# A two-layer streaming encoder on one Trainium2 core: modulation columns fetched by GpSimd's queue, three buffers for the halves, sums ordered behind products, steps dealt anew

## The chip, the cores and the metric

The kernel runs on one core of a Trainium2 chip. The engines of that core work from separate instruction queues and wait for each other through semaphores: TensorE (PE in the profile; PEld is its weight load), VectorE (DVE), ScalarE (ACT), GpSimd (POOL) and SyncE (SP). SP and POOL can issue transfers between the chip's memory (HBM) and the core's on-chip memory; the transfers of both run on the same 16 DMA engines. The metric is the device time of one execution in microseconds.

## The reference

The input is 512 tokens of width 2048. There are two layers. Each normalises the stream, scales and shifts it with values computed from a conditioning vector `c`, runs a mixer, normalises the result and adds it back times a gate:

```python
sc = jax.nn.silu(c)
for l in range(2):
    mod = sc @ ada_w[l] + ada_b[l]                  # 2048 -> 3 * 2048
    shift, scale, gate = split(mod, 3)
    h = rmsnorm(x, g_pre[l]) * (1 + scale) + shift
    if l == 0:
        y = mlstm_mixer(h, ...)                     # a_w_in, 8 heads, then @ a_w_out (4096 -> 2048)
    else:
        kmod = sc @ kv_ada_w + kv_ada_b             # 2048 -> 2 * 2048
        hkv = rmsnorm(x, kv_g) * (1 + kmod_scale) + kmod_shift
        k, v = split(hkv @ kv_w, 2)
        y = band_attention_mixer(h, k, v, b_w_in, b_rel, b_w_out)
    x = x + gate * rmsnorm(y, g_post[l])
```

What matters here is `sc @ ada_w`: one vector of 2048 numbers times matrices of 2048 x 6144 (twice) and 2048 x 4096, all in float32. It is a matrix-vector product, 128 MB of matrix that is read once.

## The kernel before

**Matrix products.** All products are float32 in three parts: each operand is split into a high part (rounded by ScalarE's cast) and a low part (VectorE's subtraction), and TensorE adds high times high, high times low and low times high. The weights come in the order in which they are used, in pieces of 128 x 1024 numbers (512 KB): SP's queue loads a piece (`raw_load`, L227; tile `wr`), ScalarE casts it (`wh`, L211), VectorE subtracts (`wl`, L211), and TensorE's 24 matmuls of 512 columns use it (L276). Three buffers each hold `wr`, `wh` and `wl`, so weights can be ready at most two pieces ahead of the one in use.

**Modulation.** One column of `mod` is one 128 x 2048 block of the matrix (a transposed `ada_w`), multiplied by the broadcast `sc` and summed along its row: a single VectorE instruction per block (CUSTOM_DVE_ANT_0 in the profile, ISA in the order of instructions, each followed by a short read of the sum). The first 32 columns are done at the start. 48 more, whole blocks of 1 MB (tile `ada`), run in the background of the first three heads of layer 0: `background(n)` sums what was loaded before and loads the next one, two or three blocks, into three buffers. The last 48 are done in halves of 128 x 1024 (512 KB, tile `adh`) during the output product of layer 0 (`a_w_out`), with the half of `sc` that belongs to them in a tile `scH` of its own (`half_sums_step`, L1071 to L1088): 96 halves, two to a step, in two buffers. A step first sums the two halves that the step before loaded, then loads two more.

**Where the steps sit.** The output product runs over four groups of 512 columns; the first three take 16 pieces each, the last is done twice, for two token pairs. A table of k indices deals a step to a piece: every second piece in the first group, 15 pieces of 16 in the second and third, four in the first half of the last. The remaining seven steps lie in the key projections (`proj_s` on `kv_w`), after the values.

**What sets the order.** A scheduler orders each engine's instructions by the place where the program issues them; `high_priority(AHEAD)` lets the preparation of weights go ahead of its place, and `pin` keeps an instruction in the order of the program among the pinned ones. In this kernel the loads of columns are pinned in SP's queue, together with those of weights, and the sums are pinned on VectorE. An engine runs its queue in order: VectorE cannot subtract a weight piece while the sum in front of it waits for its block, and SP cannot issue a load while the load in front of it waits for a buffer.

**Other names.** `ps_y` are the sums of the output product, `y` its input tiles (fetched from scratch as `yr`), `sqy` the squares that empty a bank of sums (L996) behind `y` (L995). `xr` are rows of the input for the residual (L1011), `xn` normalised rows before they are turned (L1034), both in the pool `t2` of seven buffers of 2 KB a partition. `ps_s`, `e` and L800 are the scores of an mLSTM head.

Of the kernel before, what the change touches and what calls it, by code (L numbers as in the profile page):

```python
# [9 lines left out]
F32 = mybir.dt.float32  # L10
# [144 lines left out]
def hybrid_trunk(ctx, tc, xT, xN, c, adaT, cols, wst, wg, ext, kc, out):  # L155
# [9 lines left out]
    def pool(name, bufs=1, **kw):  # L165
        return tc.tile_pool(name=name, bufs=bufs, reuse_waits="tile", **kw)
# [31 lines left out]
    def col(i):  # L198
        return cl[:, i : i + 1]
# [30 lines left out]
    def wpiece(mat, groups=(), pl=None, bufs=(2, 2), early=False):  # L230
# [41 lines left out]
                out.append((sh, sl))  # L272
        return out

    def mm(ps, a, b, start, stop):
        return nc.tensor.matmul(ps, a, b, start=start, stop=stop)  # L276

    def mm3(ps, ah, al, bh, bl, start, stop):
        mm(ps, ah, bh, start, False)
# [209 lines left out]
    acp = hst.enter_context(pool("acc"))  # L489
    st = ExitStack()  # L490
    sp = st.enter_context(pool("start"))
    def ada_load(i, p, n, pin=lambda ins: ins, parts=1, js=None):

        w = D // parts
        js = range(parts) if js is None else js
        at = p.tile([P, w * len(js)], F32, tag="ada", name=f"ada{i}_{js[0]}", bufs=n)
        for j in js:
            c = (j - js[0]) * w
            pin(nc.sync.dma_start(at[:, c : c + w], adaT[i, :, j * w : (j + 1) * w]))
        return i, at, w, js  # L500

    def ada_sum(i, at, w, js, pin=lambda ins: ins, sc=None):
        for j in js:
            c = at[:, (j - js[0]) * w : (j - js[0] + 1) * w]
            pin(nc.vector.tensor_tensor_reduce(  # L505
                c, c, (sc or scB)[:, j * w : (j + 1) * w], 1.0, mod[:, i : i + 1] if j else col(CB + i),
                ALU.mult, ALU.add, mod[:, i : i + 1]
            ))
# [229 lines left out]
    pending = list(cols_left)  # L738
    loaded = []

    def background(n):

        for a in loaded:
            ada_sum(*a, tc.keep_in_program_order)
        loaded.clear()
        for b, i in enumerate(pending[:n]):
            loaded.append(ada_load(i, *((ap_, 2) if b < 2 else (bp, 1)), tc.keep_in_program_order))
        del pending[:n]

    def add_at(at, more):  # L750
# [204 lines left out]
    kst = ExitStack()  # L955
    kp = kst.enter_context(pool("kp", bufs=KT))
    tst = ExitStack()
    tp = tst.enter_context(pool("t2", bufs=7, side="right"))
    cqst = ExitStack()
    cp = cqst.enter_context(pool("cq"))  # L960
    rst = ExitStack()
# [98 lines left out]
    def rows(g, ms, xs, at={}, pl=None):  # L1060
        ps = [newp(f"ps_y0_{g}_{m}") for m in ms]
        proj_b("a_w_out", xs, ps, ms=ms, kts=32, at=at)
        with tc.high_priority(AHEAD):
            for p, m in zip(ps, ms):
                yt[m].append((pl or rp).tile([P, S], F32, tag="t" if pl else "r", name=f"y{m}_{g}"))
                evac(p, m, g, yt[m][g])
# [4 lines left out]
    def half_sums_step():  # L1071

        for i, j, a in halves:
            pin(nc.vector.tensor_tensor_reduce(  # L1076
                a, a, sc[1], 1.0, mod[:, i : i + 1] if j else col(CB + i), ALU.mult, ALU.add, mod[:, i : i + 1]
            ))
        halves.clear()
        for i, j in cols_left[:2]:  # L1080
            d = slice(j * 2 * S, (j + 1) * 2 * S)
            if sc[0] != j:
                sc[:] = j, cp.tile([P, 2 * S], F32, tag="sc", name=f"scH{i}_{j}")
                pin(nc.sync.dma_start(sc[1], csc[0, d].partition_broadcast(P)))
            a = cp.tile([P, 2 * S], F32, tag="adh", name=f"adh{i}_{j}", bufs=2)
            pin(nc.sync.dma_start(a, adaT[i, :, d]))
            halves.append((i, j, a))
        del cols_left[:2]  # L1088

    def steps_at(*ks):  # L1090
        return {k: half_sums_step for k in ks}

    gate_row(0, 0)
    rows(0, range(4), y_tile, steps_at(*range(2, 32, 4)))
    for g in (1, 2):
        gate_row(0, g)
        rows(g, range(4), ys, steps_at(*range(0, 30, 2)))
    gate_row(0, 3)
    rows(3, PAIRS[0], ys, steps_at(2, 10, 18, 26), tp)
    at = {2: lambda: residual(0), 4: lambda: residual(1)}  # L1100
    at |= {14 + 4 * i: lambda i=i: turned(0, [i]) for i in range(4)}
    rows(3, PAIRS[1], ys, at)
# [46 lines left out]
    for pair, ms in enumerate(PAIRS):  # L1149
        for g in range(2):  # L1150
            turn = {2 + 4 * i: lambda i=i: turned(1, [i]) for i in range(4)} if pair == 0 and g == 1 else {}
            if pair:
                turn = {k: input_sums for k in (2, 6, 12)}
            values(g, ms, turn)
    rst.close()
    zst = ExitStack()
    zp = zst.enter_context(pool("zp", bufs=2, side="right"))
    zxst = ExitStack()
    zx = zxst.enter_context(pool("zx", side="right"))
    for i in range(KT // 2):  # L1160
        z = zp.tile([P, 4, 256], F32, tag="z", name=f"zk{i}")
        ready = len(hs)
        at = {2: input_sums} if ready < KT // 2 else {}
        if i == 0:
            amul_cols(2, 48 + KT, GPRE + KT)
        if 0 < i:
            at[1] = half_sums_step
        assert ready == KEY_PAIRS[i]
        proj_s("kv_w", hkv, hs, ready, z[:, 0:2, :], z[:, 2:4, :], f"k{i}", zx, (2, 2), at, True, BANKS[i % 2])
        nc.sync.dma_start(ksc[i].rearrange("p a t -> p (a t)"), z.rearrange("p a t -> p (a t)"))  # L1170
    assert not cols_left and not halves
    zxst.close()
    cqst.close()
    kst.close()
    ast = ExitStack()
    kq = ast.enter_context(pool("kq"))
# [255 lines left out]
```

## Time and profile before

| | before |
|---|---|
| median of 3 runs | 2781.33 us (2780.82 to 2786.57) |
| the profiled execution | 2783.93 us, its span 2781.8 us |
| mean granted TensorE clock | 0.997 |
| TensorE busy | 2733.4 us (98%) |
| VectorE busy | 2281.7 us (82%) |
| ScalarE busy | 1402.9 us (50%) |
| GpSimd busy | 0.2 us, 4 instructions |
| DMA, SP's queue | 504.71 MB, 53.9% of 16 engines |
| DMA, GpSimd's queue | none |

TensorE is the engine with most work, and its idle time is 48 us in all, so what an edit can win is bounded by when and why TensorE waits. The view by stage (busy time of every engine in given stretches) finds where; the view of waits and the timeline of a few microseconds tell why. A busy share of a transfer queue is the share of the time of all 16 DMA engines.

### The profile page before, as it was taken

To read this page: it belongs to the slowest core of one execution; us is meant where nothing else is said; L and a number is where in the kernel's file an instruction comes from. 1 tells how busy PE (TensorE), PEld (TensorE's weight loads), DVE (VectorE), ACT (ScalarE), POOL (GpSimd) and SP (SyncE) were. 2 spreads that over 40 slices of the span, in tenths; PEclk is the share of its full clock that TensorE was granted. 3 is DMA by queue.
4 is the path that set the end of the run, shared out by engine and by line. 5 is a ranking of instruction groups with operands and counts; after the bars stand their busy time and mean duration, and the time that the engine had idled before them with its cause. 6 is when DMAs were issued, how large, how long until landed. Compare 5 with 4: busy or idle time off the path is not lost.

```text
span 2781.8 us, 44822 instructions
## 1 busy us (share of the span) xinstructions
PE 2733.4 (98%) x17551; PEld 2485.8 (89%) x17551; DVE 2281.7 (82%) x3655; ACT 1402.9 (50%) x2011; POOL 0.2 (0%) x4
## 2 busy tenths in 40 slices
PE   8999999999999999999999989899999999999998
PEld 6887888899999999999998868677998899999887
DVE  8977979989899898998987555677997788989625
ACT  4243533556565565555655211377534566666523
POOL 0000000000000000000000000000000000000000
PEclk9999999999999999999999999999999999999999
DMA  9757787223333233332338777889655544444455
GB/s 368 293 202 266 255 330 254 95 95 121 114 108 116 94 122 115 107 116 95 121 122 277 247 248 251 272 297 301 202 189 192 178 129 125 123 130 129 167 160 177
DMA packets 158095, 507.57 MB, mean 182 GB/s; under 512 B 16902, under 2 KB 30758, under 8 KB 147386
## 3 DMA queue, kind: packets, MB, share of 16 engines
q1 hardware_dynamic: 157882, 504.71, 53.9%
q8 instruction: 137, 2.24, 0.3%
q14 instruction: 76, 0.61, 0.1%
HBM read 471.03 MB, written 38.85 MB: 183 GB/s over the span
## 4 chain that ended last, share of the span: by engine, by line
PE 81%; DMA 10%; DVE 5%; issue 2%; ACT 1%; SPq 0%; DVEq 0%; ACTq 0%
PE ps_y L276 10%; DMA adh<-in_adaT 6%; PE ps_azo L276 5%; PE ps_czo L276 5%; PE ps_dzo L276 5%; PE ps_kv L276 4%; PE ps_az L276 3%; PE ps_cz L276 3%; PE ps_dz L276 3%; PE ps_v L276 3%; PE ps_l L276 3%; PE ps_bzo L276 3%; PE ps_o L276 3%; PE ps_s L276 2%; PE ps_czq L276 2%
## 5 line engine op out<-in xcount | busy, mean ns | idle before, releaser
L211 ACT CAST wh<-wr 128x1024 fp32r<-128x1024 f32 (+1 forms) x528 | 545.7, 1036 | 590.0 <-PE ps_y L276 253.6
L211 DVE TENSOR_TENSOR wl<-wr,wh 128x1024 fp32r<-128x1024 f32 (+1 forms) x528 | 633.4, 1202 | 178.1 <-ACT wh L211 176.7
L276 PE MATMUL ps_y<-wh,y 128*128 128x512 f32 x1536 | 478.7, 392 | 13.2 <-ACT sqy L996 13.1
L211 ACT CAST wsh<-ws 128x768 fp32r<-128x768 f32 (+1 forms) x272 | 222.5, 818 | 418.9 <-issue 131.8
L276 PEld LDWEIGHTS ps_y<-wh,y 128*128 128x128 f32 x1536 | 289.3, 189 | 73.7 <-ACT sqy L996 14.0
L211 DVE TENSOR_TENSOR wsl<-ws,wsh 128x768 fp32r<-128x768 f32 (+1 forms) x272 | 253.8, 933 | 89.0 <-ACT wsh L211 84.2
L276 PE MATMUL ps_y<-wl,y 128*128 128x512 f32 x768 | 301.7, 393 | 7.9 <-DVE wl L211 7.9
L505 DVE CUSTOM_DVE_ANT_0 ada<-ada,scB,cl 128x2048 f32<-128x2048 f32 (+1 forms) x80 | 185.2, 2319 | 20.3 <-DMA ada<-in_adaT 19.7
L250 DVE TENSOR_TENSOR ws<-wr 128x512 f32<-128x512 f32 (+1 forms) x272 | 181.0, 670 | 4.7 <-DMA wr<-in_wst 4.5
L276 PEld LDWEIGHTS ps_y<-wl,y 128*128 128x128 f32 x768 | 145.0, 189 | 42.4 <-DVE wl L211 12.5
L276 PE MATMUL ps_kv<-wh,hkv 128*128 128x512 f32 x512 | 159.9, 392 | 0.0
L276 PE MATMUL ps_v<-wh,h 128*128 128x512 f32 x384 | 120.2, 390 | 0.0
L252 DVE TENSOR_TENSOR ws<-wr 128x256 f32<-128x256 f32 (+1 forms) x272 | 110.8, 412 | 2.8
L276 PEld LDWEIGHTS ps_kv<-wh,hkv 128*128 128x128 f32 x512 | 95.4, 188 | 19.3
L251 DVE TENSOR_TENSOR wr<-ws,wr 128x256 f32<-128x256 f32 (+1 forms) x272 | 110.5, 411 | 1.9
L1076 DVE CUSTOM_DVE_ANT_0 adh<-adh,scH,cl 128x1024 f32<-128x1024 f32 x48 | 61.4, 1283 | 52.4 <-DMA adh<-in_adaT 52.0
L276 PE MATMUL ps_kv<-wl,hkv 128*128 128x512 f32 x256 | 100.0, 390 | 0.2 <-DVE wl L211 0.2
L1076 DVE CUSTOM_DVE_ANT_0 adh<-adh,scH,mod 128x1024 f32<-128x1024 f32 x48 | 61.6, 1283 | 45.7 <-DMA adh<-in_adaT 45.5
L276 PE MATMUL ps_l<-h,wh 128*128 128x512 f32 x320 | 98.5, 390 | 0.0
L276 PEld LDWEIGHTS ps_v<-wh,h 128*128 128x128 f32 x384 | 72.0, 188 | 14.8
L276 PE MATMUL ps_azo<-h,wh 128*128 128x256 f32 (+1 forms) x404 | 82.1, 294 | 0.0
L276 PE MATMUL ps_v<-wl,h 128*128 128x512 f32 x192 | 75.1, 391 | 0.0
(435 smaller groups left out, 7222.3 us busy)
## 6 DMA issues: line engine op xcount, KB each, us to landing
wr<-in_wst SPq DMA_DIRECT2D x498, 512.0 KB, 3.7
ada<-in_adaT SPq DMA_DIRECT2D x78, 1024.0 KB, 7.1
adh<-in_adaT SPq DMA_DIRECT2D x96, 512.0 KB, 4.8
xt<-nsc SPq DMA_DIRECT2D x48, 256.0 KB, 4.5
wr<-in_wst SPq DMA_DIRECT2D x26, 384.0 KB, 3.8
yr<-ysc SPq DMA_DIRECT2D x28, 256.0 KB, 5.4
ysc<-zo SPq DMA_DIRECT2D x24, 256.0 KB, 3.9
bsc<-in_ext SPq DMA_DIRECT2D x16, 320.0 KB, 5.8
```

What stands on the lines that cost most here:

```text
L211: ins = nc.scalar.copy(hi, src), nc.vector.tensor_tensor(lo, src, hi.bitcast(F32), op=ALU.subtract)
L250: nc.vector.tensor_tensor(t[:, : 2 * w], r[:, w : 3 * w], r[:, : 2 * w], op=ALU.subtract)
L251: nc.vector.tensor_tensor(r[:, w : 2 * w], t[:, w : 2 * w], r[:, :w], op=ALU.add)
L252: nc.vector.tensor_tensor(t[:, 2 * w :], r[:, 3 * w :], r[:, w : 2 * w], op=ALU.subtract)
L276: return nc.tensor.matmul(ps, a, b, start=start, stop=stop)
L505: pin(nc.vector.tensor_tensor_reduce(c, c, (sc or scB)[:, j * w : (j + 1) * w], 1.0, mod[:, i : i + 1] if j else col(CB + i), ALU.mult, AL ...
L1076: pin(nc.vector.tensor_tensor_reduce(a, a, sc[1], 1.0, mod[:, i : i + 1] if j else col(CB + i), ALU.mult, ALU.add, mod[:, i : i + 1]))
```

## The change

- The columns are no longer loaded by SP's queue but by GpSimd's (`queue=nc.gpsimd`), pinned there, in the background blocks and in the halves.
- The halves have three buffers in place of two. A step sums the two oldest of three, then loads until three are there again; at a change of the half of `sc` it first sums what is left. The pool `t2` gives one of its seven buffers for it.
- Each sum is ordered behind the matmul that the program issued last before it (`paced`): an edge for the scheduler only, without a semaphore.
- The steps are dealt anew: 11 in the first group (8 before), 16 in the second and third (15), five in the first half of the last (4), two in the first value product (none), none in the key projections (7).

```diff
+    product = [None]
+
     def mm(ps, a, b, start, stop):
-        return nc.tensor.matmul(ps, a, b, start=start, stop=stop)
+        product[0] = nc.tensor.matmul(ps, a, b, start=start, stop=stop)
+        return product[0]
...
-            pin(nc.sync.dma_start(at[:, c : c + w], adaT[i, :, j * w : (j + 1) * w]))
+            pin(queue.dma_start(at[:, c : c + w], adaT[i, :, j * w : (j + 1) * w]))
...
+    def paced(ins):
+
+        behind(ins, product[0])
+        return pin(ins)
+
     def background(n):
 
         for a in loaded:
-            ada_sum(*a, tc.keep_in_program_order)
+            ada_sum(*a, paced)
         loaded.clear()
         for b, i in enumerate(pending[:n]):
-            loaded.append(ada_load(i, *((ap_, 2) if b < 2 else (bp, 1)), tc.keep_in_program_order))
+            loaded.append(ada_load(i, *((ap_, 2) if b < 2 else (bp, 1)), pin, queue=nc.gpsimd))
...
-    tp = tst.enter_context(pool("t2", bufs=7, side="right"))
+    tp = tst.enter_context(pool("t2", bufs=6, side="right"))
...
-        for i, j, a in halves:
-            pin(nc.vector.tensor_tensor_reduce(
-                a, a, sc[1], 1.0, mod[:, i : i + 1] if j else col(CB + i), ALU.mult, ALU.add, mod[:, i : i + 1]
+        for i, j, a, w in halves[: 2 if len(halves) > 2 or not cols_left or sc[0] != cols_left[0][1] else 0]:
+            paced(nc.vector.tensor_tensor_reduce(
+                a, a, w, 1.0, mod[:, i : i + 1] if j else col(CB + i), ALU.mult, ALU.add, mod[:, i : i + 1]
             ))
-        halves.clear()
-        for i, j in cols_left[:2]:
+            halves.pop(0)
+        while cols_left and len(halves) < 3:
+            i, j = cols_left.pop(0)
             d = slice(j * 2 * S, (j + 1) * 2 * S)
             if sc[0] != j:
+                if halves:
+                    cols_left.insert(0, (i, j))
+                    break
                 sc[:] = j, cp.tile([P, 2 * S], F32, tag="sc", name=f"scH{i}_{j}")
-                pin(nc.sync.dma_start(sc[1], csc[0, d].partition_broadcast(P)))
-            a = cp.tile([P, 2 * S], F32, tag="adh", name=f"adh{i}_{j}", bufs=2)
-            pin(nc.sync.dma_start(a, adaT[i, :, d]))
-            halves.append((i, j, a))
-        del cols_left[:2]
+                pin(nc.gpsimd.dma_start(sc[1], csc[0, d].partition_broadcast(P)))
+            a = cp.tile([P, 2 * S], F32, tag="adh", name=f"adh{i}_{j}", bufs=3)
+            pin(nc.gpsimd.dma_start(a, adaT[i, :, d]))
+            halves.append((i, j, a, sc[1]))
...
-    rows(0, range(4), y_tile, steps_at(*range(2, 32, 4)))
+    rows(0, range(4), y_tile, steps_at(0, 2, 6, 8, 12, 14, 18, 20, 24, 26, 30))
...
-        rows(g, range(4), ys, steps_at(*range(0, 30, 2)))
+        rows(g, range(4), ys, steps_at(*range(0, 32, 2)))
...
-    rows(3, PAIRS[0], ys, steps_at(2, 10, 18, 26), tp)
+    rows(3, PAIRS[0], ys, steps_at(2, 8, 14, 20, 26), tp)
...
+            elif g == 0:
+                turn = steps_at(4, 10)
...
-        if 0 < i:
-            at[1] = half_sums_step
```

The loads of halves in the second group of the output product, before, stand in SP's queue between those of weights (`wr`):

```order
L227 DMA wr_16462<-in_wst 128x1024
L1086 DMA adh_0_16278<-in_adaT 128x1024
L1086 DMA adh_0_16312<-in_adaT 128x1024
L227 DMA wr_16498<-in_wst 128x1024
L1086 DMA adh_0_16314<-in_adaT 128x1024
L1086 DMA adh_0_16348<-in_adaT 128x1024
L227 DMA wr_16534<-in_wst 128x1024
```

With the change they stand alone in GpSimd's queue, where only the load of the next `scH` comes between them:

```order
L1098 DMA adh_0_16224<-in_adaT 128x1024
L1098 DMA adh_0_16226<-in_adaT 128x1024
L1098 DMA adh_0_16260<-in_adaT 128x1024
L1096 DMA scH_1_16294<-csc 128x1024
L1098 DMA adh_1_16296<-in_adaT 128x1024
L1098 DMA adh_1_16298<-in_adaT 128x1024
L1098 DMA adh_1_16300<-in_adaT 128x1024
```

SP's queue is left with weights in that place; a weight load no longer stands behind one for a half.

On VectorE, in the same group, the order before is two sums (each with its read of the sum, left out here) and one subtraction for a weight piece:

```order
L211 TENSOR_TENSOR wl_16537<-wr_16534,wh_16536 128x1024
L1076 ISA adh_1_16422,mod<-adh_1_16422,scH_1_16384,mod 128x1024
...
L1076 ISA adh_1_16424,mod<-adh_1_16424,scH_1_16384,mod 128x1024
...
L211 TENSOR_TENSOR wl_16573<-wr_16570,wh_16572 128x1024
```

With the change it is the same, two sums to a subtraction, but the first of the two belongs to a half that was loaded two steps before:

```order
L211 TENSOR_TENSOR wl_16521<-wr_16518,wh_16520 128x1024
L1084 ISA adh_1_16408,mod<-adh_1_16408,scH_1_16294,mod 128x1024
...
L1084 ISA adh_1_16442,mod<-adh_1_16442,scH_1_16294,mod 128x1024
...
L211 TENSOR_TENSOR wl_16557<-wr_16554,wh_16556 128x1024
```

In the first head of layer 0, VectorE's order before has background sums (L505) just ahead of the scores `e` (L800) of that head:

```order
L211 TENSOR_TENSOR wl_2208<-wr_2205,wh_2207 128x1024
L505 ISA ada_0_1871,mod<-ada_0_1871,scB,cl 128x2048
...
L505 ISA ada_0_1873,mod<-ada_0_1873,scB,cl 128x2048
...
L800 SCALAR_TENSOR_TENSOR e_0_1950<-ps_s_0_1943,e_0_1950 128x512
L800 SCALAR_TENSOR_TENSOR e_1_1964<-ps_s_1_1957,e_1_1964 128x384
L800 SCALAR_TENSOR_TENSOR e_2_1979<-ps_s_2_1972,e_2_1979 128x256
L211 TENSOR_TENSOR wl_2238<-wr_2235,wh_2237 128x1024
```

With the change the sums that stand there are those of three earlier blocks (the numbers count up in the order of the program), and sums of later blocks follow the scores:

```order
L211 TENSOR_TENSOR wl_2208<-wr_2205,wh_2207 128x1024
L508 ISA ada_0_1801,mod<-ada_0_1801,scB,cl 128x2048
...
L508 ISA ada_0_1835,mod<-ada_0_1835,scB,cl 128x2048
...
L808 SCALAR_TENSOR_TENSOR e_0_1950<-ps_s_0_1943,e_0_1950 128x512
L808 SCALAR_TENSOR_TENSOR e_1_1964<-ps_s_1_1957,e_1_1964 128x384
L211 TENSOR_TENSOR wl_2238<-wr_2235,wh_2237 128x1024
```

Counted by weight pieces, up to four sums have moved to a later place here; ten pieces later as many have been done as before, and from there to the last at most two or three are behind.

More of the change, by code (lines that the diff above doesn't have):

```diff
@@ L491, in hybrid_trunk, with ada_load @@
     sp = st.enter_context(pool("start"))
-    def ada_load(i, p, n, pin=lambda ins: ins, parts=1, js=None):
+    def ada_load(i, p, n, pin=lambda ins: ins, parts=1, js=None, queue=nc.sync):
         w = D // parts
@@ L1153, in hybrid_trunk @@
                 turn = {k: input_sums for k in (2, 6, 12)}
+            elif g == 0:
+                turn = steps_at(4, 10)
             values(g, ms, turn)
     rst.close()
+    assert not cols_left and not halves
+    cqst.close()
     zst = ExitStack()
@@ L1170, in hybrid_trunk @@
         nc.sync.dma_start(ksc[i].rearrange("p a t -> p (a t)"), z.rearrange("p a t -> p (a t)"))
-    assert not cols_left and not halves
     zxst.close()
-    cqst.close()
     kst.close()
```

## The prediction

> **What bounds the kernel now.** I read the view by stage first (microseconds from the start; busy time of each engine, in brackets its instructions, granted TensorE clock, busy share of the DMA engines, rate).
>
> ```profile
> core 0: us, PE busy (x) PEld busy (x) DVE busy (x) ACT busy (x) POOL busy (x), PEclk, DMA share, GB/s
> 210.00:420.00 210.00, 207.12 (x945) 168.94 (x944) 177.28 (x195) 88.19 (x117) 0.00 (x0) 1.00 0.78 284
> 540.00:1465.00 925.00, 924.97 (x7496) 915.83 (x7495) 845.49 (x1373) 529.14 (x674) 0.00 (x0) 1.00 0.35 112
> 1465.00:1565.00 100.00, 100.00 (x454) 83.22 (x453) 72.93 (x98) 43.50 (x66) 0.00 (x0) 1.00 0.81 266
> 1565.00:1660.00 95.00, 84.65 (x367) 68.06 (x365) 53.87 (x73) 15.79 (x15) 0.00 (x0) 0.98 0.71 245
> 1660.00:1760.00 100.00, 90.17 (x385) 72.78 (x385) 60.29 (x83) 20.03 (x27) 0.00 (x0) 0.96 0.77 252
> 1760.00:1850.00 90.00, 87.79 (x383) 70.98 (x383) 59.15 (x77) 47.62 (x76) 0.00 (x0) 0.98 0.89 293
> 1850.00:2015.00 165.00, 159.87 (x933) 139.23 (x932) 136.70 (x235) 117.40 (x196) 0.00 (x0) 1.00 0.79 257
> 2015.00:2125.00 110.00, 110.00 (x878) 108.18 (x877) 93.54 (x153) 39.35 (x48) 0.00 (x0) 1.00 0.51 173
> ```
>
> TensorE is busy all the time but for the output product of layer 0, from 1565 on, and a little beside it. The chain of waits, in order of time, says what ends last there: TensorE in the first group, then transfers of halves.
>
> ```profile
> 1485.27 74.40 PE ps_y L276 x328
> 1600.33 4.49 DMA adh<-in_adaT
> 1606.28 5.03 DMA adh<-in_adaT
> 1615.68 6.88 DMA adh<-in_adaT
> ```
>
> The first row gives the price of a product: 74.40 / 328 = 0.2268 us, so a piece of 24 products takes TensorE 5.44. At that price 367 and 385 products are 83.2 and 87.3 us; the two stretches lose 11.8 and 12.7, together **24.5 us**. The stretch to 1850 loses 90 - 383 x 0.2268 = 3.1. VectorE's timeline shows the loop that does it.
>
> ```profile
> 1600.22 1.22 DVE L211 TENSOR_TENSOR wl<-wr,wh 128x1024 fp32r<-128x1024 f32 x1
> 1601.70 1.28 DVE L1076 CUSTOM_DVE_ANT_0 adh<-adh,scH,cl 128x1024 f32<-128x1024 f32 x1 [0.26 <-DMA adh<-in_adaT]
> 1604.96 1.28 DVE L1076 CUSTOM_DVE_ANT_0 adh<-adh,scH,cl 128x1024 f32<-128x1024 f32 x1 [1.96 <-DMA adh<-in_adaT]
> 1606.17 1.22 DVE L211 TENSOR_TENSOR wl<-wr,wh 128x1024 fp32r<-128x1024 f32 x1
> 1608.04 1.28 DVE L1076 CUSTOM_DVE_ANT_0 adh<-adh,scH,cl 128x1024 f32<-128x1024 f32 x1 [0.65 <-DMA adh<-in_adaT]
> 1611.44 1.29 DVE L1076 CUSTOM_DVE_ANT_0 adh<-adh,scH,cl 128x1024 f32<-128x1024 f32 x1 [2.11 <-DMA adh<-in_adaT]
> 1612.65 1.22 DVE L211 TENSOR_TENSOR wl<-wr,wh 128x1024 fp32r<-128x1024 f32 x1
> 1603.02 3.58 SPq L1086 DMA_DIRECT2D adh<-in_adaT  x2
> ```
>
> A weight piece (wl) becomes ready at 1600.22, 1606.17, 1612.65: every 6.22 us, while TensorE eats one in 5.44. VectorE has only 1.22 + 2 x 1.28 = 3.78 us of work in it; the rest it waits for halves. The wait is the buffers': a half's load can start only when the sum two places before it has ended. The sum at 1601.70 ended at 1602.98, SP issued at 1603.02, the sum in that buffer began at 1608.04: a **latency L** of 5.06 from one to the other, and 5.20 for the next. With two buffers a step of two sums takes at least L + 1.28 = 6.3 to 6.5. Weights made ahead hide that until they are used up; then TensorE starves:
>
> ```profile
> 1600.00:1610.00 10.00, 10.00 (x46) 8.29 (x45) 6.46 (x10) 2.11 (x2) 0.00 (x0) 1.00 0.73 238
> 1650.00:1660.00 10.00, 3.02 (x13) 1.84 (x11) 6.47 (x10) 0.00 (x0) 0.00 (x0) 0.85 0.59 210
> 1660.00:1670.00 10.00, 9.24 (x34) 7.57 (x35) 7.11 (x11) 4.48 (x10) 0.00 (x0) 0.81 0.88 270
> 1750.00:1760.00 10.00, 4.06 (x19) 2.86 (x17) 7.60 (x11) 0.81 (x3) 0.00 (x0) 0.80 0.76 263
> ```
>
> After each of the two long gaps the granted clock is 0.80 to 0.85 and 34 products stand where 46 do, so a gap costs more than its idle time; the counts above hold both.
>
> **The change part by part.**
>
> *Three buffers.* A load now starts when the sum three places before it has ended. Three sums take at least L + 1.28, so a step of two takes (2/3)(L + 1.28). With L = 5.1 that is 4.25, under TensorE's 5.44, and the 24.5 us go, the slow clock with them. TensorE keeps being the bound until L = 6.88; the old 6.22 comes back at L = 8.05. At 5.44 us a step, two halves and one piece (1.573 MB) are 289 GB/s, above the 245 to 252 of today's rows but within what this profile moves:
>
> ```profile
> 1470.00:1480.00 10.00, 10.00 (x50) 8.32 (x50) 8.81 (x15) 9.80 (x18) 0.00 (x0) 1.00 1.00 374
> DMA to landing us min/median/max: 3.5/4.8/7.8
> adh<-in_adaT SPq DMA_DIRECT2D x18, 512.0 KB, 5.2
> ada<-in_adaT SPq DMA_DIRECT2D x78, 1024.0 KB, 7.1
> ```
>
> The second row is over all halves, the third over those of 1465 to 1565, where the engines were 81% busy: a median of 5.2 against 4.8. So the load itself adds some 0.4.
>
> *GpSimd's queue.* GpSimd issues no transfer in this trace, so what its queue adds to L is not to be seen. From below: a gain is possible, since a half no longer stands behind another load in SP's queue (the 3.58 for two issues, of which most is the wait for a buffer), but it must still wait for its buffer, so at best nothing. From above: as if the load were of 1 MB, the last row's 7.1 in place of 4.8, 2.3 us more. I take 0.7, nearer the lower end, as the move changes who issues, not the bytes: L = 5.1 + 0.4 + 0.7 = 6.2, a step 4.99 us. That leaves 0.45 us before it costs anything; at the upper end, L = 7.8, a step takes 6.05 and most of the gain is gone. The Trainium skill (DMA: Bandwidth & Descriptors, Latency and other measured facts) gives about 0.6 us to the first byte for a transfer issued by SP and about 1 us for one by GpSimd; by it the term would be an estimated 0.4, the step 4.8, the sum the same. No run here shows it yet.
>
> *A new half of scH*, four times, empties the loop: its own load and three halves at once. Today that is the chain's 6.88 us and VectorE stood 6.31 us. Two spare pieces, 10.9 us, hide it now where the loop is faster than TensorE; I keep 1.5 us. SP's queue is left to the weights, which so cannot come later than they do.
>
> *The steps dealt anew.* Three more in the first group put 6 x 1.28 = 7.7 us on VectorE, busy 72.9 of 100 there: covered. Two in the first value product put 5.1 us on it, busy 136.7 of 165: covered on average. The seven removed from the key projections (93.5 of 110 busy) relieve VectorE where TensorE is already busy 110.0 of 110: nothing.
>
> *One buffer fewer in t2.*
>
> ```profile
> 1805.56 5.87 DMA xr<-in_xN
> PE ps_x L1042 <- DVE xn L1034: 2.0, 2, 1.3
> L1034 DVE TENSOR_SCALAR xn<-y,rsn x16: 474/478/486, 1835.9 to 1910.6; 128x512 f32<-128x512 f32 x16
> ```
>
> Residual rows and turned rows share it; a row that finds no buffer is fetched later by at most a landing, 5.87 us, with VectorE queued behind it. Weights made ahead cover one such wait. I take 1 us, between none and 6. The 3.1 us of 1760 to 1850 stay.
>
> *Sums behind products* in the first head, where blocks of 2.3 us are summed.
>
> ```profile
> L505 DVE CUSTOM_DVE_ANT_0 ada<-ada,scB,cl 128x2048 f32<-128x2048 f32 (+1 forms) x80 | 185.2, 2319 | 20.3 <-DMA ada<-in_adaT 19.7
> 260.00:270.00 10.00, 7.23 (x39) 6.04 (x38) 6.02 (x7) 2.20 (x4) 0.00 (x0) 1.00 0.70 263
> PE ps_s L276 <- DVE e L800: 2.8, 1, 2.8
> 300.00:310.00 10.00, 10.00 (x46) 8.29 (x45) 10.00 (x10) 2.89 (x4) 0.00 (x0) 1.00 0.53 159
> ```
>
> Today TensorE waits 2.8 us at 265 for scores (e) that stand on VectorE behind two sums whose blocks are late. Now the sums ahead of the scores are of blocks that were loaded sooner: that wait can go. But up to four sums, 9.3 us, move to where VectorE is busy 10.00 of 10; two spare pieces (10.9) cover them just. Bounds: -2.8 and, with half the cover used already, +4; I take -1.
>
> *Sum.* -24.5 + 1.5 + 1 - 1 = -23 us against the profiled execution, 2783.9 (span 2781.8), hence 2760.9 there; the median of the runs shown, 2781.3, is 2.6 below it, so **2758 us**.
>
> **The rivals.**
>
> *A latency in between* (18%). GpSimd's queue adds 2 us, L = 7.5, a step 5.85: 32 steps of the second and third group lag 0.41 each, 13.2 us, 6 for an scH with no cover, less 10.9 of spare pieces: 8 us stay of the 24.5, about 2766, to 2776 at the upper bound. For it: most transfers take longer when more are in flight. Against: 0.7 us of room in L.
>
> *Slower* (14%). One mechanism: halves come through GpSimd so late that three buffers are worse than two were. It decides from L = 8.05. At the 9.05 us that the chain shows for the slowest load of a block a step takes 6.89, 32 steps lag 46 us, less 10.9, plus the 6 and some 5 for the slow clock: 46 lost in place of 24.5, **2803 us**.
>
> ```profile
> 247.07 9.05 DMA ada<-in_adaT
> ```
>
> How it could come about: GpSimd must write each load's descriptors, and if any VectorE instruction kept it from that, a sum and a subtraction (2.5 us) would be added, L = 8.7. The Trainium skill (SBUF — State Buffer, SBUF: two separate sides) limits the lock to VectorE's two-port modes. The rows agree with such a mode in one kind alone: L1034 takes 478 ns for 512 columns, and its 16 lie after 1835, when few halves are left. By that rule L grows by half a microsecond there and not in the loop. So the chance stays low.
>
> *The change doesn't do what it says* (8%). If the rate is the limit, a third load in flight only makes all three longer and a step stays at 6.2 us: 2781. For it: 0.77 busy at 252 GB/s. Against: 374 GB/s at 1.00.
>
> **How the numbers follow.** The forecast has 60%, with its own range of 2750 (the 2.8 and 1.5 saved as well, and part of the 3.1) to 2765 (both small costs at their bounds). With the case in between 78% for faster; 8% for the same, 14% slower; a change within 0.2%, 5.6 us, can't be told from none. Eight times in ten the time lies in 2749 to 2779: that leaves out the slower case and half of the unchanged one.
>
> **What would show it.** Right: in the second group sums two to a step of 5.44 us, no wait of TensorE for wl or sqy between 1565 and 1760, a clock of 1.00 there, and halves landing in under 6.9 us from the end of the sum three places before. Wrong: a step still near 6.2 (rate or queue), VectorE waiting for ada in the first heads longer than today's 19.7 us, or waits for xr and xn above 6 us between 1780 and 1960.

## The result, and the profile after

The change made no difference that can be measured: 2784.97 us in the median of 12 runs (2778.97 to 2795.41) against 2785.30 for the kernel before on the same chip (12 runs, 2779.15 to 2787.45), a ratio of 1.0004 [0.9991, 1.0018] (of all the runs, not of the two medians). The forecast was 2758 us. The profiled span is 2779.2 us in place of 2781.8. Two things happened, and they cancel: the output product gained as forecast, though less, and the first heads lost.

The view by stage of the changed kernel (columns as in the prediction):

```profile
core 0: us, PE busy (x) PEld busy (x) DVE busy (x) ACT busy (x) POOL busy (x), PEclk, DMA share, GB/s
210.00:420.00 210.00, 204.88 (x913) 166.38 (x912) 170.58 (x185) 85.95 (x114) 18.59 (x35) 0.98 0.72 265
420.00:540.00 120.00, 112.98 (x532) 95.35 (x532) 108.82 (x164) 49.57 (x76) 5.84 (x11) 0.97 0.59 206
1565.00:1660.00 95.00, 95.00 (x421) 78.69 (x420) 64.81 (x88) 21.16 (x26) 18.07 (x35) 1.00 0.82 286
1660.00:1760.00 100.00, 93.07 (x401) 75.91 (x400) 65.09 (x91) 20.03 (x27) 18.59 (x35) 0.97 0.81 278
1760.00:1850.00 90.00, 89.09 (x390) 72.88 (x391) 63.88 (x85) 49.12 (x79) 5.31 (x10) 0.97 0.91 308
```

From 1565 to 1660 TensorE is now full, 421 products at clock 1.00 where 367 stood. From 1660 on it still idles 6.9 of 100 us. Against that, 210 to 420 shows 913 products for 945 before, and 420 to 540 stands at 112.98 busy; before, that stretch was all but full:

```profile
420.00:540.00 120.00, 119.85 (x585) 101.18 (x584) 114.13 (x188) 57.50 (x86) 0.00 (x0) 1.00 0.53 181
```

Two groups in the chain of waits give the sum of it; both kernels have them in the same places. A pair of matmul groups of the third head, before and then after:

```profile
595.32 3.62 PE ps_n L276 x22
```

```profile
608.92 3.62 PE ps_n L278 x22
```

and the last product of layer 1, before and then after:

```profile
2609.69 163.93 PE ps_y L276 x723
```

```profile
2606.57 163.93 PE ps_y L278 x723
```

So the changed kernel was 13.6 us late by 600, and 3.1 us early by 2600: the part in between won 16.7 us.

**Where the heads lose.** The longest waits of TensorE in the changed kernel:

```profile
PE ps_n L278 <- DVE so L940: 7.0, 1, 7.0
PE ps_s L278 <- DVE e L808: 4.9, 1, 4.9
```

VectorE's timeline shows the second of them (start, duration, line, operation, in brackets the idle time before it and what ended that; the short reads of the sums are left out):

```profile
257.85 2.35 DVE L508 CUSTOM_DVE_ANT_0 ada<-ada,scB,cl 128x2048 f32<-128x2048 f32 x1
260.12 1.22 DVE L211 TENSOR_TENSOR wl<-wr,wh 128x1024 fp32r<-128x1024 f32 x1
263.16 2.35 DVE L508 CUSTOM_DVE_ANT_0 ada<-ada,scB,cl 128x2048 f32<-128x2048 f32 x1 [1.82 <-DMA ada<-in_adaT]
267.71 2.35 DVE L508 CUSTOM_DVE_ANT_0 ada<-ada,scB,cl 128x2048 f32<-128x2048 f32 x1 [2.19 <-DMA ada<-in_adaT]
269.99 1.15 DVE L808 SCALAR_TENSOR_TENSOR e<-ps_s,e 128x512 f32<-128x512 f32 x2
```

Two sums in a row wait for their blocks, 1.82 and 2.19 us, with the scores `e` queued behind them. Why the blocks are late is seen 30 us earlier, in the first load that GpSimd issues here:

```profile
231.75 0.53 POOL L502 DMA_DIRECT2D ada<-in_adaT  x1 [77.97 <-DVE mod L508]
```

It had to wait for the sum that frees its buffer, and that sum now stands behind later products: it began at 229.12, in the kernel before at 205.12:

```profile
229.12 2.33 DVE L508 CUSTOM_DVE_ANT_0 ada<-ada,scB,cl 128x2048 f32<-128x2048 f32 x1
```

```profile
205.12 2.34 DVE L505 CUSTOM_DVE_ANT_0 ada<-ada,scB,cl 128x2048 f32<-128x2048 f32 x1
```

The four sums that were moved are not only late themselves; each holds a buffer, so the loads behind them are late too, the first by 24 us (231.75 for 207.50). VectorE and the DMA engines are idle first and crowded later:

```profile
210.00:220.00 10.00, 10.00 (x40) 4.65 (x39) 1.43 (x2) 1.52 (x3) 0.00 (x0) 1.00 0.15 54
260.00:270.00 10.00, 5.80 (x30) 4.92 (x28) 5.99 (x8) 1.54 (x2) 1.06 (x2) 1.00 0.93 366
270.00:280.00 10.00, 9.27 (x31) 7.71 (x32) 8.94 (x13) 2.90 (x6) 1.59 (x3) 0.66 0.64 217
420.00:430.00 10.00, 3.60 (x22) 3.14 (x21) 7.73 (x10) 1.87 (x4) 1.06 (x2) 0.85 0.83 315
430.00:440.00 10.00, 9.38 (x38) 8.06 (x39) 8.09 (x11) 2.47 (x4) 1.06 (x2) 0.81 0.96 344
```

VectorE works 1.43 of 10 us at 210. At 260 and 420 TensorE misses 4.2 and 6.4 us, and after each the granted clock falls: 31 and 38 products in 10 us where a full stretch has 46. At 420 the loss is larger. The second head's first products `ps_n` started at 418.02, before at 414.62, so 3.4 of the 13.6 us were lost by then and 10.2 came after. VectorE at that place, in the changed kernel:

```profile
422.40 2.35 DVE L508 CUSTOM_DVE_ANT_0 ada<-ada,scB,cl 128x2048 f32<-128x2048 f32 x1 [2.27 <-DMA ada<-in_adaT]
424.68 2.35 DVE L211 TENSOR_TENSOR wl<-wr,wh 128x1024 fp32r<-128x1024 f32 x2
426.95 0.68 DVE L921 TENSOR_TENSOR so<-so,sz 128x512 f32<-128x512 f32 x1
427.55 2.35 DVE L508 CUSTOM_DVE_ANT_0 ada<-ada,scB,cl 128x2048 f32<-128x2048 f32 x1
429.82 1.40 DVE L940 SCALAR_TENSOR_TENSOR so<-ps_n,cl,so 128x512 f32<-128x512 f32 x2
```

A sum that waited 2.27 us, two subtractions and another sum stand ahead of the row (`so`, L940) for which TensorE waits 7.0. Before, that row started at 417.20:

```profile
417.20 1.40 DVE L932 SCALAR_TENSOR_TENSOR so<-ps_n,cl,so 128x512 f32<-128x512 f32 x2
```

### The profile page after: what moved, and what is told of

Its sections match the earlier page's. It is cut to its first block, busy times and chain, and to the rows that moved or that the text cites. A ratio compares the mean times of both kernels' runs of the same rounds, so it can differ in the third digit from the quotient of the medians.

```text
span 2779.2 us, 44879 instructions
## 1 busy us (share of the span) xinstructions
PE 2734.5 (98%) x17551; PEld 2490.8 (90%) x17551; DVE 2283.3 (82%) x3655; ACT 1401.0 (50%) x2011; POOL 78.9 (3%) x152
## 4 chain that ended last, share of the span: by engine, by line
PE 76%; issue 12%; DVE 5%; DMA 4%; POOL 2%; ACT 1%; SPq 0%; POOLq 0%; DVEq 0%; ACTq 0%
PE ps_y L278 8%; PE ps_azo L278 5%; PE ps_czo L278 5%; PE ps_dzo L278 5%; PE ps_kv L278 4%; PE ps_az L278 3%; PE ps_cz L278 3%; PE ps_dz L278 3%; PE ps_l L278 3%; PE ps_bzo L278 3%; PE ps_v L278 3%; PE ps_czq L278 2%; PE ps_cv L278 2%; PE ps_dzq L278 2%; PE ps_azq L278 2%
## 5 line engine op out<-in xcount | busy, mean ns | idle before, releaser
L508 DVE CUSTOM_DVE_ANT_0 ada<-ada,scB,cl 128x2048 f32<-128x2048 f32 (+1 forms) x80 | 185.2, 2319 | 28.5 <-DMA ada<-in_adaT 28.3
```

Of the source, the lines that this page charges most:

```text
L508: pin(nc.vector.tensor_tensor_reduce(c, c, (sc or scB)[:, j * w : (j + 1) * w], 1.0, mod[:, i : i + 1] if j else col(CB + i), ALU.mult, AL ...
```

## The experiments

All twelve kernels were timed in five rounds against the kernel before on the same chip; ratios are to that, with the 95% interval. E1 to E4, then E5, E6, E7 and E10, then the rest ran on three chips, so between these groups only the ratios compare. The last columns are from the profiled execution of each: the start of the row `ps_n ... x22` shown above, and the time from the first matmul of layer 0's output product to the start of the row `ps_y ... x723` of layer 1, which holds the whole output product. 0.001 is 2.8 us.

| kernel | ratio | ps_n at | product to layer 1's end |
|---|---|---|---|
| before | 1 | 595.3 | 1141.6 |
| the change | 1.0004 [0.9991, 1.0018] | 608.9 | 1125.0 |
| E1 blocks not paced | 0.9945 [0.9933, 0.9957] | 595.7 | 1125.6 |
| E2 blocks by SP, paced | 0.9959 [0.9945, 0.9974] | 597.8 | 1123.1 |
| E3 blocks as before | 0.9951 [0.9937, 0.9964] | 593.3 | 1129.1 |
| E4 blocks changed alone | 1.0067 [1.0048, 1.0086] | 607.1 | 1138.9 |
| E5 = E3, halves by SP | 0.9902 [0.9886, 0.9917] | 592.1 | 1109.1 |
| E6 = E3, halves not paced | 1.0014 [1.0003, 1.0025] | 595.7 | 1140.4 |
| E7 = E3, one switch of scH | 0.9917 [0.9903, 0.9931] | 591.9 | 1112.8 |
| E10 = E3, two buffers | 1.0107 [1.0087, 1.0127] | 593.2 | 1171.9 |
| E11 = E5, one switch of scH | 0.9899 [0.9884, 0.9914] | 593.1 | 1111.7 |
| E13 = E5, two buffers | 1.0072 [1.0058, 1.0087] | 593.5 | 1161.0 |
| E14 = E5, halves not paced | 0.9943 [0.9929, 0.9957] | 600.0 | 1125.0 |
| E15 = E3, four buffers | 0.9979 [0.9970, 0.9988] | 594.6 | 1135.7 |

The nine kernels from E3 on that leave the first heads alone have `ps_n` between 591.9 and 600.0. So one execution's value is good to some 4 us, and the 608.9 and 607.1 lie outside.

**E1 to E4: which edit costs in the first heads.** "Paced" is the place behind the latest product. E1 takes it from the sums of blocks, E2 takes GpSimd's queue from their loads, E3 both; E4 is the kernel before with both, and its old halves.

```diff
# E1
-            ada_sum(*a, paced)
+            ada_sum(*a, pin)
# E2
-            loaded.append(ada_load(i, *((ap_, 2) if b < 2 else (bp, 1)), pin, queue=nc.gpsimd))
+            loaded.append(ada_load(i, *((ap_, 2) if b < 2 else (bp, 1)), pin))
```

> The changed kernel, but the sums of the 48 background blocks are only pinned, not ordered behind a product; they stay on GpSimd's queue. In the changed kernel the first heads end 13.6 us later than before (a pair of products ps_n of 3.6 us starts at 608.9 against 595.3) and the output product is about 17 us shorter. Theory A, the order of the sums costs the 13.6 us: VectorE's order is that of before again, no gap of TensorE at 260 to 280 beyond the 2.8 us of before and none at 420 to 430, ps_n near 595, the time 2770 to 2773, 12 to 15 us below before. Theory B, GpSimd's queue brings the blocks too late: the gaps stay, ps_n near 609, the time stays at 2785.

> The changed kernel, but the background blocks are loaded by SP's queue as before; their sums stay ordered behind products. Theory A, the order of the sums costs the 13.6 us: nothing is won, ps_n stays near 609, the time 2783 to 2788 (some more if weights wait behind blocks in SP's queue). Theory B, GpSimd's queue costs it: ps_n near 595, the time 2770 to 2773.

> The changed kernel, but the background blocks as before: SP's queue, sums only pinned. Only the edits to the halves are left. Both theories: ps_n near 595 and the output product as in the changed kernel, the time 2766 to 2771. It fixes what the halves' part of the change is worth alone: 17 us by the two traces; if it is under 8, the shift in the first heads has part in the gain seen later.

> The kernel before, with only the background blocks changed: GpSimd's queue and sums ordered behind products; the halves as before. Both theories: the loss of the first heads alone, ps_n near 609, the time 2796 to 2801, slower than before by 11 to 16 us. If it is within 5 us of before, the two parts of the change do not simply add.

The halves' edits alone (E3) are worth 0.49%, the blocks' edits alone (E4) cost 0.67%; together they would give 1.0018, and the change measured 1.0004. In E4 the two waits of the changed kernel come back with nothing else changed:

```profile
PE ps_n L278 <- DVE so L940: 6.5, 1, 6.5
PE ps_s L278 <- DVE e L808: 4.0, 1, 4.0
```

Its profiled execution, 2792.77 us, is faster than the median, 2799.57, and shows a loss of 11.8 us in the heads; the rest of E4's loss is not seen in it.

Neither edit costs alone: E1 came out as theory A had it and E2 as theory B, and E1, E2 and E3 cannot be told apart. E2's sums are just as late at first, the first at 229.03, and VectorE waited 26.7 us for blocks (28.3 in the changed kernel and 16.8 in E3). But the last two sums ahead of the scores waited less, 0.25 and 1.20 us in place of 1.82 and 2.19, and from 229 on eight sums in all stood ahead of the scores, not nine:

```profile
260.25 2.35 DVE L508 CUSTOM_DVE_ANT_0 ada<-ada,scB,cl 128x2048 f32<-128x2048 f32 x1 [0.25 <-DMA ada<-in_adaT]
263.82 2.35 DVE L508 CUSTOM_DVE_ANT_0 ada<-ada,scB,cl 128x2048 f32<-128x2048 f32 x1 [1.20 <-DMA ada<-in_adaT]
266.10 1.48 DVE L808 SCALAR_TENSOR_TENSOR e<-ps_s,e 128x512 f32<-128x512 f32 x3
```

and TensorE waited 0.9 us for them in place of 4.9. In the second head the row `so` started at 419.00, behind one sum that waited 0.30 us, in place of 429.82. The scheduler had dealt the instructions of these stretches in another order; the loads in another queue are all that differs between the two programs. That the order is what keeps E2 cheap is read from these rows and was not tried by itself.

**E5: GpSimd's queue for the halves.** E3, with scH and halves issued by SyncE (SP).

```diff
-                pin(nc.gpsimd.dma_start(sc[1], csc[0, d].partition_broadcast(P)))
+                pin(nc.sync.dma_start(sc[1], csc[0, d].partition_broadcast(P)))
...
-            pin(nc.gpsimd.dma_start(a, adaT[i, :, d]))
+            pin(nc.sync.dma_start(a, adaT[i, :, d]))
```

> Blocks of the first head as before; the halves of the output product keep three buffers, the new dealing and their place behind a product, but they and scH are issued by SyncE's queue again. Ratios are to the kernel before; e3_blocks_as_before, the same kernel with GpSimd's queue, stood at 0.9951. Theory A (the queue matters: on SyncE a half's load is issued only when the weight loads ahead of it in the queue have got their buffers): 0.9965 to 1.000, five to fourteen us above e3, with longer waits of VectorE for adh than e3's 65.5 us. Theory B (the third buffer and the dealing are all there is in it, GpSimd's queue buys nothing): 0.994 to 0.996, halves landing in about 5 us after issue in place of 6.0.

Neither: 0.9902, half a per cent below E3 where A had put it above. Issued by SP, the loop keeps up through the whole product. The same stretch in E3 and then in E5:

```profile
1700.00:1750.00 50.00, 43.62 (x185) 35.35 (x184) 32.69 (x45) 11.07 (x17) 9.03 (x17) 0.95 0.79 278
```

```profile
1700.00:1750.00 50.00, 50.00 (x222) 41.41 (x221) 36.99 (x48) 15.13 (x20) 0.00 (x0) 1.00 0.88 298
```

Three rows of each kernel show why. In E3 a sum and the next load of GpSimd (timeline), and the time from issue to landing of all halves from 1500 to 1800 (view by tile):

```profile
1573.75 1.28 DVE L1084 CUSTOM_DVE_ANT_0 adh<-adh,scH,cl 128x1024 f32<-128x1024 f32 x1 [1.31 <-DMA adh<-in_adaT]
1575.45 0.54 POOL L1098 DMA_DIRECT2D adh<-in_adaT  x1 [3.22 <-DVE mod L1084]
```

```profile
DMA to landing us min/median/max: 3.9/6.0/10.1
```

and the same in E5:

```profile
1575.99 1.28 DVE L1084 CUSTOM_DVE_ANT_0 adh<-adh,scH,cl 128x1024 f32<-128x1024 f32 x1
1577.30 0.33 SPq L1098 DMA_DIRECT2D adh<-in_adaT  x1
```

```profile
DMA to landing us min/median/max: 4.2/5.4/7.4
```

The sum ends at 1575.03, and GpSimd starts to issue 0.42 us later; SP does so 0.03 us after the sum's end. From the issue on, the median is 6.0 against 5.4 us and the slowest 10.1 against 7.4. So L is about 6.4 with GpSimd, with a tail far above the limit of 6.88, and about 5.4 with SP, with a tail of 7.4. The longer landing is not the queue's by itself: with two buffers GpSimd's halves landed in a median of 4.3 us and SP's in 4.9 (E10, then E13, again from 1500 to 1800):

```profile
DMA to landing us min/median/max: 3.7/4.3/7.7
DMA to landing us min/median/max: 3.6/4.9/6.9
```

So it comes with three halves in flight beside the weights; why SP's order then keeps landings shorter was not tried. The slowest stand where scH and three halves are asked for at once; E7, with one such place, has 9.0 at most.

The queue costs in a second way, by when it issues. GpSimd's queue does not stand behind SP's: it issued scH and three halves at 1462.5, when head 7's rows were still to be read back; SP issued its own first at 1478.95. SP's reads of those rows in E3, and TensorE's wait behind them:

```profile
1464.83 17.11 SPq L985 DMA_DIRECT2D yr<-ysc  x13
1475.36 3.38 PE L278 MATMUL ps_n<-p,v 128*128 128x512 f32 x11 [4.05 <-ACT dd L927]
```

In E5 the same thirteen reads took 12.16 us and that wait is gone:

```profile
1463.57 12.16 SPq L985 DMA_DIRECT2D yr<-ysc  x13
```

That wait is 0.8 to 4.0 us in the eight kernels whose halves go through GpSimd's queue, E3's being the longest, and at most 0.5 in the six that use SP's.

**E6 and E14: the place behind the product for the halves' sums,** taken away with GpSimd's queue (E6) and with SP's (E14).

```diff
-            paced(nc.vector.tensor_tensor_reduce(
+            pin(nc.vector.tensor_tensor_reduce(
```

> Blocks as before; halves with three buffers on GpSimd's queue, new dealing, but their sums only kept in program order on VectorE, no longer placed behind the latest product. Theory A (the steps of the output product lie so regularly that the scheduler puts the sums in the same places either way): within 0.001 of e3, 0.994 to 0.996. Theory B (placing a sum behind a product costs here as it did in the first heads, where late sums made late loads): 2 to 5 us less than e3, 0.993 to 0.9945. Theory C (without it sums move ahead of work that TensorE waits for): above 0.997.

> As e5_halves_by_SP, but the halves' sums are only kept in program order on VectorE, not behind the latest product (as e6_halves_not_paced, which was 17 us above e3). Theory A (what the place behind a product buys is the order on VectorE, where else a sum that waits for its half stands ahead of a weight's rounding that TensorE waits for; that comes with either queue): 0.994 to 0.998. Theory B (it matters only where halves come late, as with GpSimd): 0.990 to 0.992.

C for E6 and A for E14: without it 17 and 11 us are lost. In the product it does what it should. In E14, where it is gone, a sum that waited 5.37 us stands alone ahead of a weight piece, though the halves come by SP:

```profile
1653.36 1.28 DVE L1084 CUSTOM_DVE_ANT_0 adh<-adh,scH,mod 128x1024 f32<-128x1024 f32 x1 [5.37 <-DMA adh<-in_adaT]
1654.57 1.22 DVE L211 TENSOR_TENSOR wl<-wr,wh 128x1024 fp32r<-128x1024 f32 x1
```

**E7 and E11: one switch of scH in place of three,** by the order of the halves; E7 on E3, E11 on E5.

```diff
-    cols_left = [(48 + i, j) for j in range(2) for i in range(2 * KT)] + [(80 + i, j) for j in range(2) for i in range(KT)]
+    cols_left = [(48 + i, j) for j in range(2) for i in range(3 * KT)]
```

> Blocks as before; halves as in the changed kernel, but all 48 first halves of the rows come before all 48 second halves, so the multiplier scH is loaded twice in place of four times, and the buffers are run empty once in place of three times. Theory A (what the output product still loses is the emptying at the switches: TensorE of e3 stood 7.7 us between 1650 and 1750): one switch is left, 5 to 8 us less than e3's 0.9951, so 0.992 to 0.9935, and no stretch of TensorE's idle time at 1700 to 1750. Theory B (the gaps come from the rate at which the halves arrive, and the switches merely lie there): within 2 us of e3, 0.9945 to 0.996, with the gaps elsewhere.

> Blocks as before, halves by SyncE's queue with three buffers and behind products (as e5_halves_by_SP, 0.9902), and the multiplier scH loaded twice in place of four times (as e7_one_switch). Theory A (the switches cost only because GpSimd's halves came late; with SyncE TensorE of e5 is busy 50.0 of 50 us in every stretch from 1500 to 1800, so there is nothing left to gain): within 0.0008 of e5, 0.9894 to 0.991. Theory B (the two edits add, 0.5% and 0.35%): 0.986 to 0.988.

Theory A both times. With GpSimd's queue it saves 0.34%, and TensorE's gaps at 1650 to 1750 are all but gone (1660 to 1760 is 99.24 of 100 us busy); with SP's queue it saves nothing. In the changed kernel the second switch looks like this, first on GpSimd, then on VectorE:

```profile
1696.21 0.53 POOL L1096 DMA_DIRECT2D scH<-csc  x1 [6.04 <-DVE mod L1084]
1696.77 1.64 POOL L1098 DMA_DIRECT2D adh<-in_adaT  x3
1704.66 1.28 DVE L1084 CUSTOM_DVE_ANT_0 adh<-adh,scH,cl 128x1024 f32<-128x1024 f32 x1 [6.29 <-DMA adh<-in_adaT]
```

The last sum before it ended at 1695.80, the next began at 1704.66: 8.9 us for one round, with weights made ahead worth 10.9 us only where the loop has had time to make them.

**E10 and E13: two buffers,** on E3 and on E5.

```diff
-        for i, j, a, w in halves[: 2 if len(halves) > 2 or not cols_left or sc[0] != cols_left[0][1] else 0]:
+        for i, j, a, w in halves[: 2 if len(halves) > 1 or not cols_left or sc[0] != cols_left[0][1] else 0]:
...
-        while cols_left and len(halves) < 3:
+        while cols_left and len(halves) < 2:
...
-            a = cp.tile([P, 2 * S], F32, tag="adh", name=f"adh{i}_{j}", bufs=3)
+            a = cp.tile([P, 2 * S], F32, tag="adh", name=f"adh{i}_{j}", bufs=2)
```

> Blocks as before; halves on GpSimd's queue, behind products, in the new dealing of steps, but with two buffers in place of three. Theory A (the prediction's round trip: with two buffers a step of two sums cannot be shorter than landing and one sum, here 6.0 + 0.5 + 1.28 = 7.8 us by e3's landing, against 5.44 us of products): the gain of e3 is gone, 0.999 to 1.006, and VectorE waits for adh over 95 us. Theory B (the dealing, which begins earlier and leaves fewer halves to the middle heads, brought the gain): 0.994 to 0.997.

> As e5_halves_by_SP with two buffers for halves in place of three; queue, place behind products and dealing as there. Theory A (the round trip of two buffers: landing 5.4 + 1.28 = 6.7 us against 5.44 us of products a step; it is the third buffer that removes the stalls, whichever queue): 0.999 to 1.003, VectorE waiting for adh about 95 us. Theory B (place and dealing carry the gain, and the third buffer only makes up for GpSimd's longer way): 0.990 to 0.993.

Theory A, and more than it said: the third buffer is worth 43 us with GpSimd's queue and 47 with SP's. The weight pieces of E13 in the second group become ready every 6.35 us (1612.73 to 1638.12, four steps):

```profile
1612.73 1.22 DVE L211 TENSOR_TENSOR wl<-wr,wh 128x1024 fp32r<-128x1024 f32 x1
...
1638.12 1.22 DVE L211 TENSOR_TENSOR wl<-wr,wh 128x1024 fp32r<-128x1024 f32 x1
```

which is the prediction's round trip, 6.3 to 6.5. E10's steps are no longer, 6.17 us (1628.21 to 1646.73, three steps), where its expectation had 7.8: its halves landed in 4.3 us, not in 6.0. E13 is slower than the kernel before, which also has two buffers and SP's queue: the new dealing, the place behind products and the tile taken from t2 together cost 20 us where the loop is slower than TensorE. They were not separated there, and the old dealing was not tried with three buffers.

**E15: four buffers,** on E3; the pool t2 has four tiles of six to make room.

```diff
-    tp = tst.enter_context(pool("t2", bufs=6, side="right"))
+    tp = tst.enter_context(pool("t2", bufs=4, side="right"))
...
-        while cols_left and len(halves) < 3:
+        while cols_left and len(halves) < 4:
...
-            a = cp.tile([P, 2 * S], F32, tag="adh", name=f"adh{i}_{j}", bufs=3)
+            a = cp.tile([P, 2 * S], F32, tag="adh", name=f"adh{i}_{j}", bufs=4)
```

> As e3_blocks_as_before (GpSimd's queue, 0.9951) with four buffers for halves; the pool t2 has four tiles in place of six to make room, which may cost the heads 1 to 4 us by itself and is seen where the output product starts. Theory A (GpSimd's queue costs by its longer way and the spread of it, 4.0 to 11.3 us a landing in the changed kernel, and another buffer covers that): the output product's stretches 1500 to 1750 full as in e5, 0.990 to 0.993 with t2's cost. Theory B (GpSimd's halves cost because the weight loads of SyncE no longer take turns with them and the 16 DMA engines are shared otherwise; a buffer does not mend the rate): 0.9945 to 0.998, gaps of TensorE as in e3.

By the ratio B, by the trace A. With GpSimd's queue and four buffers VectorE waited 11.9 us for halves in place of E3's 65.5, and the stretch with E3's gaps is full. What was won is lost after it, in the residual rows that share t2:

```profile
1700.00:1750.00 50.00, 50.00 (x222) 41.44 (x221) 35.25 (x47) 13.11 (x19) 8.80 (x17) 1.00 0.86 299
1800.00:1850.00 50.00, 44.15 (x204) 34.52 (x203) 32.72 (x51) 33.20 (x62) 0.00 (x0) 1.00 0.76 242
1850.00:1900.00 50.00, 43.51 (x178) 32.46 (x176) 28.88 (x46) 32.64 (x67) 0.00 (x0) 0.93 0.82 265
```

In E3 these last two are 48.71 and 48.78 busy. VectorE waits up to 2.93 us for a row `xr` there, and TensorE 6.6 us in all for `xn` (2.5 in E3); that t2 is the cause is read from these waits and was not tried by itself. So the full stretch shows latency as GpSimd's cost, not the rate: with a fourth load in flight the same queue kept TensorE full there, at 299 GB/s.

## Why the prediction was wrong, point by point

**The step that failed** is "Sums behind products in the first head": "Bounds: -2.8 and, with half the cover used already, +4; I take -1." Measured, by the same matmul group before and after, it was +13.6, and E3 and E4 put all of it on the two block edits. The step counted how much sum time moves to a later place, 9.3 us, and set it against the 10.9 us of weights made ahead. It did not follow the moved sum to what it frees. Each of the four holds a buffer for 24 us or more longer, its next load starts late, and so the sums that come to stand ahead of the scores are again of late blocks, which the step had excluded ("of blocks that were loaded sooner"). It also stopped at the first head, and 10.2 of the 13.6 us came in the second. What GpSimd's queue does to the blocks had no term, though the same edit moves them. Their landing is not it: from 195 to 285 a block took a median of 5.8 us by GpSimd, and 6.2 by SP before. E1 and E2 show that the two edits cost only together, and E2 that late loads alone cost nothing that was measured. What remains between E2 and the changed kernel is the order on VectorE, nine sums for eight ahead of the scores and `so` at 429.82 for 419.00; why the two edits together deal it so stays open. The prediction's own sign did show: VectorE waited 28.3 us for `ada`, longer than 19.7. The +4 was no bound either: after the gaps of 4.2 and 6.4 us the clock was 0.66 and 0.81 for the next 10 us, so that they cost more than their idle time, and there were two of them.

**Three buffers: right in mechanism.** The loss of 1565 to 1660 went to nothing, clock included, and E10 and E13 show that the round trip is what bounds two buffers. Its size fits where the halves come by SP: E5's profiled execution, its fastest, wins 32.6 us from the output product on, and by the medians E5 wins 27.1 in all. That is the forecast 24.5 and a part of the 3.1 and 5.1 (165 - 159.87) that TensorE lost between 1760 and 2015, where E5 still idles 1.2 and 2.4. In the changed kernel 16.6 came.

**GpSimd's queue** was mis-sized in its spread. The term gave L = 6.2; by E3's rows it is 0.42 + 6.0 = 6.4, still under the limit of 6.88. But a limit on the median is not enough: single landings of up to 10.1 us lie above it, and what two pieces ready ahead do not cover, TensorE waits for. That a half "no longer stands behind another load in SP's queue" was the reason given for a possible gain. E5 shows the queue as a whole as a loss of 14 us, and a part of it, 4 us at head 7 in E3's profiled execution, comes just from that: SP's queue had held the first four loads back until the rows were in. The prediction also had SP's queue left to weights that "cannot come later"; the rows that SP reads there did come later. From the end of a sum to the end of the next issue the rows show 0.96 us with GpSimd (0.42 + 0.54) and 0.36 with SP (0.03 + 0.33), 0.6 us more. The Trainium skill (DMA: Bandwidth & Descriptors, Latency and other measured facts) gives the first byte at about 1 us for GpSimd and about 0.6 for SP, an estimated 0.4 more. No row here shows the first byte by itself.

**A new half of scH** was mis-sized: "I keep 1.5 us". E7 wins 9.5 us by taking two switches away, in a kernel with GpSimd's queue. The two spare pieces were there only where L leaves room to make them; with SP's they are, and E11 shows the switch at nothing.

**The steps dealt anew, t2:** covered, as far as E5 shows; 1800 to 1850 is 48.81 of 50 busy with six tiles. With four it costs (E15).

**The rivals.** "Latency in between" (18%) named the right queue and about the right loss in the product, 8 us stay of 24.5. The number is in part luck: it had L = 7.5 and a step of 5.85 throughout, and the runs show a median L of 6.4 and a tail. No rival lay in the first heads.

**The better version.** The changed kernel with the blocks as before and the halves by SP (E5) takes 2752.62 us where the kernel before takes 2779.70, a ratio of 0.9902 [0.9886, 0.9917]: what remains of the change is the third buffer, with one tile fewer in t2, the place behind products in the halves, and the dealing.

## What to carry to other kernels

When an instruction that reads a buffer is moved later, follow the buffer: the next load into it moves as well, and so does whoever waits for that load. Late loads alone need not cost (E2); what is queued behind the instruction that waits for them decides. A ring of buffers has to be judged by the slow landings, not by the median, since an engine with two pieces ahead has little to spare. And an edit that acts in two places (here a queue and an order, used in the heads and in the product) is two edits with two prices: the same place behind a product was worth 11 to 17 us in the product and had a part in a loss of 14 in the heads.

## What was not expected of the hardware

- A 512 KB load issued by GpSimd took a median of 6.0 us and up to 10.1 to land, by SP 5.4 and up to 7.4, with the same bytes in the same product and three buffers (E3, E5). With two buffers it was the other way, 4.3 by GpSimd and 4.9 by SP (E10, E13).
- A queue of its own gave GpSimd's loads a head start over SP's that was not wanted: thirteen reads by SP took 17.11 us (E3) in place of 12.16 (E5).
- In the heads as well, gaps of TensorE were followed by a lower granted clock in the next ten microseconds: 0.66 and 0.81 in the changed kernel, 0.85 and 0.83 in E4. In the changed kernel, 4.2 us of idle time at 260 came with 31 products for 46 in the 10 us that followed.
